# Batched 90-degree rotation on one core: one 8 KB-row slab at each end of the order instead of two at the start, and stores that are not held back

## The chip, the cores and the metric

The kernel runs on one core of a Trainium2 chip. The metric is the time of one execution on the device, in microseconds (us). The kernel before takes 122.95 us, the median of three runs (122.94 to 122.95).

## The reference

The input is a batch of 32 x 3 images of 256 x 256 float32 values, 25.17 MB. Every image is turned by 90 degrees clockwise:

```python
def reference(x):
    return np.rot90(x, k=-1, axes=(-2, -1)).astype(np.float32)
```

Nothing is calculated. Each value is read from HBM (the chip's main memory) once and written back once, elsewhere: 50.33 MB in all.

## The kernel before

All images together are 24,576 rows of 256 values (1 KB each). The kernel cuts them into twelve **slabs** of 2,048 rows, 2 MB each, which is 16 KB on each of the 128 partitions of SBUF (the on-chip memory). All twelve slabs have a place of their own in SBUF, so that no buffer is used twice. The slabs form five **groups** of `sizes = (2, 2, 2, 4, 2)` slabs, in the tiles `groups[0]` to `groups[4]`.

**Loads.** SP, an engine that here only issues transfers, issues every load and every store, in the order of the program, into a single queue. Group 0 is loaded in a form of its own (lines 52 to 56): its two slabs lie as rows of 8 KB on each partition. The second slab comes first, as two transfers of 1 MB (line 55), then the first slab as one transfer of 2 MB (line 56). Groups 1 to 4 are loaded by lines 57 to 66 with rows of 16 KB (32 KB in group 3), one transfer of 2 MB per slab. The last of them is cut into two of 1 MB: line 63, whose instruction is kept in the variable `mark`, and line 64. That makes 14 loads.

**Turning.** VectorE (DVE in the profile) turns the data with its transpose instruction, 24 times 128 partitions x 2,048 values. `turn_slab` (lines 68 to 72) handles the two slabs of group 0 with two transposes each. The slab that comes first is turned into the two halves of `spare`, which lie in PSUM (a small second memory of the core); the other one is turned into the place that the first has left (lines 75 and 76). ScalarE (ACT) then copies `spare` into the place that the second slab has left (line 78). `turn_group` (lines 80 to 98) turns a group of slabs in place: a quarter of the data is transposed into a side buffer, `extra` or `spare` (line 88), the other three quarters inside the group's own tile (line 93), and ACT copies the side buffer back (line 98).

**Stores.** Each group leaves in two transfers, one with the even partitions and one with the odd ones (lines 104 to 113): 2 MB each, 4 MB each in group 3. That makes 10 stores. The first store has an extra dependency on `mark` (lines 107 to 109): SP waits in front of it until the load of line 63 has landed.

All instructions of SP run in order: what stands behind a waiting instruction waits too. The framework gives the transfers eight completion counters (semaphores) in turn, and each transfer waits until the one eight places ahead of it, which used the same counter, has landed.

Of the kernel before, what the change touches and what calls it, by code (L numbers as in the profile page):

```python
# [1 line left out]

# [4 lines left out]


@with_exitstack  # L10
def kernel(
    ctx: ExitStack,
    tc: tile.TileContext,
    x: bass.AP,
    out: bass.AP,
):

    nc = tc.nc
    fp32 = mybir.dt.float32

    B, C, H, W = x.shape
    P = nc.NUM_PARTITIONS
    R = 16  # L30
    E = R * W
    hw = R // 2
    low, high = slice(0, hw), slice(hw, R)

    rows_in = x.rearrange("b c h w -> (b c h) w")
    rows_out = out.rearrange("b c h w -> (b c h) w")

    sizes = (2, 2, 2, 4, 2)
    first = [sum(sizes[:n]) for n in range(len(sizes))]
    groups = [  # L40
        ctx.enter_context(tc.tile_pool(name=f"group{n}", bufs=1)).tile([P, s, E], fp32, name=f"u{n}")
        for n, s in enumerate(sizes)
    ]
    psum = ctx.enter_context(tc.tile_pool(name="psum", bufs=1, space=bass.MemoryType.PSUM))
    spare = [psum.tile([P, E // 2], fp32, name=f"spare{h}") for h in range(2)]
    extra = ctx.enter_context(tc.tile_pool(name="extra", bufs=1)).tile([P, E // 2], fp32, name="extra")

    def rows_of(rows, n):
        return rows[first[n] * P * R : (first[n] + sizes[n]) * P * R]


    ld = rows_of(rows_in, 0).rearrange("(s i p r) w -> s i p (r w)", s=2, i=2, p=P)
    home = [groups[0][:, s].rearrange("p (i f) -> p i f", i=2) for s in range(2)]
    for i in range(2):
        nc.sync.dma_start(out=home[0][:, i], in_=ld[1, i])  # L55
    nc.sync.dma_start(out=home[1], in_=ld[0].transpose([1, 0, 2]))
    for n in range(1, len(sizes)):
        I = sizes[n]
        ld = rows_of(rows_in, n).rearrange("(a i m r) w -> i m a (r w)", a=2, i=I, m=P // I)
        to = groups[n].rearrange("p s f -> p (s f)").rearrange("p (a f) -> p a f", a=2)  # L60
        for i in range(I):
            if (n, i) == (len(sizes) - 1, I - 1):
                mark = nc.sync.dma_start(out=to[i::I, 0], in_=ld[i][:, 0])
                nc.sync.dma_start(out=to[i::I, 1], in_=ld[i][:, 1])
            else:
                nc.sync.dma_start(out=to[i::I], in_=ld[i])

    def turn_slab(src, dsts):
        s = src.rearrange("p (i r g c) -> p c r g i", i=2, r=R // 2, c=R)
        for h, d in enumerate(dsts):  # L70
            d = d.rearrange("p (c k r) -> p c r k", c=hw, r=R // 2)[:, :, ::-1, ::-1]
            nc.vector.transpose(out=d, in_=s[:, h * hw : (h + 1) * hw])  # L72

    u = groups[0]
    turn_slab(u[:, 0], spare)
    turn_slab(u[:, 1], [u[:, 0, : E // 2], u[:, 0, E // 2 :]])
    for h in range(2):
        nc.scalar.copy(out=u[:, 1, h * E // 2 : (h + 1) * E // 2], in_=spare[h])  # L78

    def turn_group(n, held):  # L80
        I = sizes[n]
        T = I // 2
        K = W // (R * T)
        u = groups[n].rearrange("p s f -> p (s f)")
        src = u.rearrange("p (a t r g c) -> p t c r g a", a=2, t=T, r=R, c=R)
        dst = u.rearrange("p (i c k t r) -> p t c r k i", i=I, c=R, k=K, t=T)[:, ::-1, :, ::-1, ::-1, :]
        for t in range(T):
            nc.vector.transpose(  # L88
                out=held[t].rearrange("p (i c k r) -> p c r k i", i=I, c=hw, k=K)[:, :, ::-1, ::-1, :],
                in_=src[:, t, low, low])  # L90
        for c, r in ((low, high), (high, high), (high, low)):
            for t in range(T):
                nc.vector.transpose(out=dst[:, t, c, r], in_=src[:, t, c, r])  # L93
        back = u.rearrange("p (i c k t r) -> p t i c k r", i=I, c=R, k=K, t=T)[:, ::-1]
        for t in range(T):
            kept = held[t].rearrange("p (i c k r) -> p i c k r", i=I, c=hw, k=K)
            for i in range(I):
                nc.scalar.copy(out=back[:, t, i, low, :, high], in_=kept[:, i])  # L98

    for n, held in enumerate(([extra], [spare[1]], spare, [extra]), 1):  # L100
        turn_group(n, held)


    st = rows_of(rows_out, 0).rearrange("(s i m r) w -> i m s (r w)", s=2, i=2, m=P // 2)
    for a in range(2):
        put = nc.sync.dma_start(out=st[a], in_=groups[0][a::2])
        if a == 0:
            tc.add_manual_dep(put.ins, mark.ins.name, mybir.DependencyInfo(
                mybir.DependencyClass.Sync, mybir.DependencyReason.SCHED_ONLY), reason="stores after loads")
    for n in range(1, len(sizes)):  # L110
        st = rows_of(rows_out, n).rearrange("(a i m r) w -> a m i (r w)", a=2, i=sizes[n], m=P // 2)
        for a in range(2):
            nc.sync.dma_start(out=st[a], in_=groups[n][a::2])


# [1 line left out]
_INS = ['x']  # L117
_OUTS = [((32, 3, 256, 256), 'float32')]


# [23 lines left out]
```

## Time and profile before

| what | value |
|---|---|
| median of the runs shown | 122.95 us (122.94 to 122.95) |
| the profiled execution's own time | 122.88 us |
| its span, first to last instruction | 121.1 us |
| VectorE busy | 87.4 us in 24 instructions |
| ScalarE busy | 14.9 us in 17 instructions |
| moved by the 16 DMA engines | 50.33 MB, 416 GB/s over the span |
| line 72, transposes into `spare` | 2, mean 3,586 ns |
| line 72, transposes into the group's tile | 2, mean 3,988 ns |
| line 78, copies by ScalarE from `spare` | 2, mean 1,870 ns |
| line 98, copies by ScalarE from a side buffer | 14, mean 605 to 1,043 ns by shape |

The profile page names an engine, a line, an operation and its tiles in each row, then how many there were and how long they took. The span is cut into 40 slices of 3 us, with a digit for each engine's busy share in tenths and the GB/s that the DMA engines moved. Other views of the same trace give the instructions in order of time, the waits by engine, and busy times in chosen stretches; "share" of the DMA there is the mean over the 16 DMA engines. "SPq" is the sequencer of SP, where the transfers are issued: an issue takes half a microsecond or so, and the transfer lands much later.

### The profile page before, as it was taken

Reading aid. Unit: us, or ns where it says so; the run is one execution under the profiler, and the core shown is the slowest. Engines: PE = TensorE matmul, PEld = TensorE weight load, DVE = VectorE, ACT = ScalarE, POOL = GpSimd, SP = SyncE. Lnnn points to the kernel's source line nnn. Section 1 sums busy time; section 2 is a strip of 40 time slices with the busy share of each in tenths; the row PEclk is TensorE's granted clock in tenths of the full one; section 3 lists DMA queues with packets and bytes.
Section 4 is the critical chain, followed back from the end, with each engine's and each line's share of the span. In section 5 each row is a group of like instructions: output and inputs, shape, how many; then the busy total and the mean of one; then the engine's idle time right before and its main releaser. Section 6 shows DMA issues by size and latency. Waiting matters only on the chain.

```text
span 121.1 us, 131 instructions
## 1 busy us (share of the span) xinstructions
DVE 87.4 (72%) x24; ACT 14.9 (12%) x17; POOL 0.2 (0%) x4
## 2 busy tenths in 40 slices
DVE  0039999999999999999999999999999600000000
ACT  0000400380005100060000000318000330000000
POOL 0000000000000000000000000000000000000000
DMA  2999999999989898999999999999999999999994
GB/s 89 428 428 422 452 433 433 433 433 433 520 346 520 346 520 346 428 422 411 433 433 428 433 433 428 417 417 433 428 433 433 433 433 433 433 433 433 433 422 184
DMA packets 3456, 50.33 MB, mean 416 GB/s; under 512 B 384, under 2 KB 384, under 8 KB 384
## 3 DMA queue, kind: packets, MB, share of 16 engines
q1 hardware_dynamic: 3456, 50.33, 97.6%
HBM read 25.17 MB, written 25.17 MB: 416 GB/s over the span
## 4 chain that ended last, share of the span: by engine, by line
DVE 66%; issue 6%; DMA 6%; ACT 1%; ACTq 1%; SPq 0%; DVEq 0%
DVE u L93 39%; DVE spare L88 9%; DVE extra L88 6%; DVE u L72 6%; DVE spare L72 6%; DMA u<-in_x_dram 6%; ACT u L98 1%; ACTq L139 1%; SPq L55 0%; DVEq L88 0%; DVEq L72 0%
## 5 line engine op out<-in xcount | busy, mean ns | idle before, releaser
L93 DVE STREAM_TRANSPOSE u<-u 128x2048 f32<-128x2048 f32 x15 | 54.4, 3649 | 0.4
L72 DVE STREAM_TRANSPOSE spare<-u 128x2048 f32<-128x2048 f32 x2 | 7.1, 3586 | 8.1 <-DMA u<-in_x_dram 8.1
L98 ACT COPY u<-spare 128x512 f32<-128x512 f32 (+1 forms) x10 | 6.0, 687 | 38.5 <-DVE u L93 38.5
L88 DVE STREAM_TRANSPOSE spare<-u 128x2048 f32<-128x2048 f32 x3 | 10.7, 3588 | 0.0
L72 DVE STREAM_TRANSPOSE u<-u 128x2048 f32<-128x2048 f32 x2 | 7.8, 3988 | 0.0
L88 DVE STREAM_TRANSPOSE extra<-u 128x2048 f32<-128x2048 f32 x2 | 7.8, 3896 | 0.0
L98 ACT COPY u<-extra 128x1024 f32<-128x1024 f32 x4 | 4.0, 1043 | 22.8 <-DVE u L93 22.8
L78 ACT COPY u<-spare 128x2048 f32<-128x2048 f32 x2 | 3.6, 1870 | 8.7 <-DVE u L72 8.7
L78 ACT ACT_TABLE_LOAD x1 | 1.3, 1283 | 13.0 <-DMA u<-in_x_dram 13.0
L128 POOL MEMSET const-uint8-127<- 128x1 uint8 x1 | 0.1, 103 | 0.0
L128 POOL MEMSET const-bfloat16-1.0<- 128x1 bf16 x1 | 0.1, 102 | 0.0
L128 POOL MEMSET const-float32-0.0<- 128x1 f32 x1 | 0.1, 99 | 0.2 <-issue 0.2
L128 POOL MEMSET const-float32-1.0<- 128x1 f32 x1 | 0.1, 99 | 0.0
## 6 DMA issues: line engine op xcount, KB each, us to landing
u<-in_x_dram SPq DMA_DIRECT2D x10, 2048.0 KB, 30.4
out_dram<-u SPq DMA_DIRECT2D x8, 2048.0 KB, 18.2
out_dram<-u SPq DMA_DIRECT2D x2, 4096.0 KB, 21.1
u<-in_x_dram SPq DMA_DIRECT2D x4, 1024.0 KB, 20.5
```

The costliest lines, as they stand in the source:

```text
L72: nc.vector.transpose(out=d, in_=s[:, h * hw : (h + 1) * hw])
L78: nc.scalar.copy(out=u[:, 1, h * E // 2 : (h + 1) * E // 2], in_=spare[h])
L88: nc.vector.transpose(out=held[t].rearrange("p (i c k r) -> p c r k i", i=I, c=hw, k=K)[:, :, ::-1, ::-1, :], in_=src[:, t, low, low])
L93: nc.vector.transpose(out=dst[:, t, c, r], in_=src[:, t, c, r])
L98: nc.scalar.copy(out=back[:, t, i, low, :, high], in_=kept[:, i])
L128: nc = _bacc.Bacc("TRN2", target_bir_lowering=False, num_devices=1)
L139: with _tile.TileContext(nc) as tc:
```

## The change

The twelve slabs are grouped as `(1, 2, 2, 4, 2, 1)`. The first and the last group hold one slab each in the form with 8 KB rows; the first is loaded as two transfers of 1 MB and the last as one of 2 MB. Both are turned into the two halves of `spare`, and ScalarE copies them back into their own place, where before only one of two slabs went that way. The last load of 16 KB rows is no longer cut in two. The dependency of the first store on `mark` is gone. The two single slabs are stored as two transfers of 1 MB each.

```diff
-    sizes = (2, 2, 2, 4, 2)
+    sizes = (1, 2, 2, 4, 2, 1)
...
+    for n, I in enumerate(sizes):
+        u = groups[n].rearrange("p s f -> p (s f)")
+        if I == 1:
+            ld = rows_of(rows_in, n).rearrange("(i p r) w -> i p (r w)", i=2, p=P)
+            to = u.rearrange("p (i f) -> p i f", i=2)
+            if n:
+                nc.sync.dma_start(out=to, in_=ld.transpose([1, 0, 2]))
+            else:
+                for i in range(2):
+                    nc.sync.dma_start(out=to[:, i], in_=ld[i])
+            continue
+        ld = rows_of(rows_in, n).rearrange("(a i m r) w -> i m a (r w)", a=2, i=I, m=P // I)
+        to = u.rearrange("p (a f) -> p a f", a=2)
+        for i in range(I):
+            nc.sync.dma_start(out=to[i::I], in_=ld[i])
-    ld = rows_of(rows_in, 0).rearrange("(s i p r) w -> s i p (r w)", s=2, i=2, p=P)
-    home = [groups[0][:, s].rearrange("p (i f) -> p i f", i=2) for s in range(2)]
-    for i in range(2):
-        nc.sync.dma_start(out=home[0][:, i], in_=ld[1, i])
-    nc.sync.dma_start(out=home[1], in_=ld[0].transpose([1, 0, 2]))
...
-            if (n, i) == (len(sizes) - 1, I - 1):
-                mark = nc.sync.dma_start(out=to[i::I, 0], in_=ld[i][:, 0])
-                nc.sync.dma_start(out=to[i::I, 1], in_=ld[i][:, 1])
...
+    def turn_slab(n):
+        u = groups[n][:, 0]
+        s = u.rearrange("p (i r g c) -> p c r g i", i=2, r=R // 2, c=R)
+        for h in range(2):
+            d = spare[h].rearrange("p (c k r) -> p c r k", c=hw, r=R // 2)[:, :, ::-1, ::-1]
             nc.vector.transpose(out=d, in_=s[:, h * hw : (h + 1) * hw])
-    u = groups[0]
-    turn_slab(u[:, 0], spare)
-    turn_slab(u[:, 1], [u[:, 0, : E // 2], u[:, 0, E // 2 :]])
-    for h in range(2):
-        nc.scalar.copy(out=u[:, 1, h * E // 2 : (h + 1) * E // 2], in_=spare[h])
+        for h in range(2):
+            nc.scalar.copy(out=u[:, h * E // 2 : (h + 1) * E // 2], in_=spare[h])
...
+    turn_slab(0)
     for n, held in enumerate(([extra], [spare[1]], spare, [extra]), 1):
         turn_group(n, held)
+    turn_slab(len(sizes) - 1)
...
-    for a in range(2):
-        put = nc.sync.dma_start(out=st[a], in_=groups[0][a::2])
-        if a == 0:
-            tc.add_manual_dep(put.ins, mark.ins.name, mybir.DependencyInfo(
-                mybir.DependencyClass.Sync, mybir.DependencyReason.SCHED_ONLY), reason="stores after loads")
+            st = rows_of(rows_out, n).rearrange("(a m r) w -> a m (r w)", a=2, m=P // 2)
+            for a in range(2):
+                nc.sync.dma_start(out=st[a], in_=groups[n][a::2, 0])
+            continue
```

More of the change, by code (lines that the diff above doesn't have):

```diff
@@ L49, in rows_of @@
         return rows[first[n] * P * R : (first[n] + sizes[n]) * P * R]
-    ld = rows_of(rows_in, 0).rearrange("(s i p r) w -> s i p (r w)", s=2, i=2, p=P)
-    home = [groups[0][:, s].rearrange("p (i f) -> p i f", i=2) for s in range(2)]
-    for i in range(2):
-        nc.sync.dma_start(out=home[0][:, i], in_=ld[1, i])
-    nc.sync.dma_start(out=home[1], in_=ld[0].transpose([1, 0, 2]))
-    for n in range(1, len(sizes)):
-        I = sizes[n]
+    for n, I in enumerate(sizes):
[9 more added lines that the diff above has]
+            continue
@@ L59 @@
         ld = rows_of(rows_in, n).rearrange("(a i m r) w -> i m a (r w)", a=2, i=I, m=P // I)
-        to = groups[n].rearrange("p s f -> p (s f)").rearrange("p (a f) -> p a f", a=2)
+        to = u.rearrange("p (a f) -> p a f", a=2)
         for i in range(I):
-            if (n, i) == (len(sizes) - 1, I - 1):
[L63 to L71, printed above, removed]
-            nc.vector.transpose(out=d, in_=s[:, h * hw : (h + 1) * hw])
-    u = groups[0]
-    turn_slab(u[:, 0], spare)
-    turn_slab(u[:, 1], [u[:, 0, : E // 2], u[:, 0, E // 2 :]])
-    for h in range(2):
-        nc.scalar.copy(out=u[:, 1, h * E // 2 : (h + 1) * E // 2], in_=spare[h])
+            nc.sync.dma_start(out=to[i::I], in_=ld[i])
@@ L98, in turn_group @@
                 nc.scalar.copy(out=back[:, t, i, low, :, high], in_=kept[:, i])
+    turn_slab(0)
     for n, held in enumerate(([extra], [spare[1]], spare, [extra]), 1):
         turn_group(n, held)
-    st = rows_of(rows_out, 0).rearrange("(s i m r) w -> i m s (r w)", s=2, i=2, m=P // 2)
-    for a in range(2):
-        put = nc.sync.dma_start(out=st[a], in_=groups[0][a::2])
-        if a == 0:
-            tc.add_manual_dep(put.ins, mark.ins.name, mybir.DependencyInfo(
-                mybir.DependencyClass.Sync, mybir.DependencyReason.SCHED_ONLY), reason="stores after loads")
-    for n in range(1, len(sizes)):
-        st = rows_of(rows_out, n).rearrange("(a i m r) w -> a m i (r w)", a=2, i=sizes[n], m=P // 2)
+    turn_slab(len(sizes) - 1)
+    for n, I in enumerate(sizes):
+        if I == 1:
+            st = rows_of(rows_out, n).rearrange("(a m r) w -> a m (r w)", a=2, m=P // 2)
+            for a in range(2):
+                nc.sync.dma_start(out=st[a], in_=groups[n][a::2, 0])
+            continue
+        st = rows_of(rows_out, n).rearrange("(a i m r) w -> a m i (r w)", a=2, i=I, m=P // 2)
         for a in range(2):
```

## The prediction

> **What bounds the kernel now.** I read the page first: busy rows, the DMA row, the queue and the chain.
>
> ```profile
> DVE 87.4 (72%) x24; ACT 14.9 (12%) x17; POOL 0.2 (0%) x4
> ...
> DMA  2999999999989898999999999999999999999994
> ...
> q1 hardware_dynamic: 3456, 50.33, 97.6%
> ...
> DVE 66%; issue 6%; DMA 6%; ACT 1%; ACTq 1%; SPq 0%; DVEq 0%
> ```
>
> The chain names VectorE, but its shares add up to 80%: it ends with the issue of the last stores, and the last fifth of the span, in which their data still moves, isn't in it. The DMA row and the queue's 97.6% name the real bound. The stretches (DVE, ACT, POOL busy, clock, DMA share, GB/s) show where the missing 2.4% lies:
>
> ```profile
> 59.00:63.00 4.00, 3.97 (x3) 0.00 (x0) 0.00 (x0) 1.00 1.01 430
> 63.00:97.00 34.00, 32.71 (x9) 5.19 (x10) 0.00 (x0) 1.00 1.00 427
> 97.00:118.00 21.00, 0.00 (x0) 0.91 (x1) 0.00 (x0) 1.00 1.02 432
> ```
>
> Further stretches of this view have a DMA share of 0.13 up to 1.9 us and of 0.00 from 120.0 us on. Between the two the engines never pause, not even at 59 to 63, where loads give way to held stores. Next, SP's waits and the issues in time:
>
> ```profile
> SPq L106 <- DMA u<-in_x_dram: 31.2, 1, 31.2
> ```
> ```profile
> 12.95 0.60 SPq L66 DMA_DIRECT2D u<-in_x_dram  x1
> ...
> 17.84 0.61 SPq L66 DMA_DIRECT2D u<-in_x_dram  x1
> ...
> 22.75 0.51 SPq L63 DMA_DIRECT2D u<-in_x_dram  x1
> 27.64 0.49 SPq L64 DMA_DIRECT2D u<-in_x_dram  x1
> ...
> 59.43 1.37 SPq L106 DMA_DIRECT2D out_dram<-u  x2
> ```
>
> Each of these four loads waits for the landing eight places ahead of it, so the issues are a clock of landings: 4.89 us per 2 MB of 16 KB rows (17.84 to 22.75 to 27.64), and 4.97 for the 8 KB slab (first slab landed 7.98, second 12.95). Line 63 lands 36.5 us after its issue (59.25), line 64 34.1 us after (61.74): 2.49 us for 1 MB. The last store lands 21.7 us after its issue at 98.6: 120.3. From 7.98 to 120.3 move 23 slabs' worth, 112.3 / 23 = 4.88 each. The time is the queue's bytes; all else only has to keep ahead of it.
>
> How far ahead it is, from VectorE's and ScalarE's instructions in time:
>
> ```profile
> 22.84 3.91 DVE L88 STREAM_TRANSPOSE extra<-u 128x2048 f32<-128x2048 f32 x1
> ...
> 81.04 3.88 DVE L88 STREAM_TRANSPOSE extra<-u 128x2048 f32<-128x2048 f32 x1
> ```
> ```profile
> 81.19 3.03 ACT L98 COPY u<-spare 128x512 f32<-128x512 f32 x6 [2.69 <-DVE u L93]
> 95.92 1.99 ACT L98 COPY u<-extra 128x1024 f32<-128x1024 f32 x2 [11.70 <-DVE u L93]
> ```
>
> Group 3, the large one, is ready at 84.2. The queue runs dry without it after all loads and six 2 MB stores: 61.74 + 6 x 4.88 = 91.0. Cover 6.8 us; for group 4 (ready 97.9, needed at 110.6) 12.7 us.
>
> **The change, part by part.**
>
> *Loads.* Thirteen instead of fourteen: two of 1 MB, ten of 2 MB with long rows, one 8 KB slab. The bytes per row form are the same (two slabs of 8 KB, six of 16 KB, four of 32 KB); the 4.97 us slab moves from second place to last. Only the cut of the last 16 KB load goes. A cut costs 2.49 - 4.89 / 2 = 0.045 us; the pair at the start (0.73 + 4.8 = 5.5 and 7.98, so 2.4 to 2.5 us each, against 4.97) says between -0.03 and nothing. I take 0.045, nearest in row length and partitions (64): -0.045. Loads end at 61.7, as before.
>
> *Stores.* Twelve instead of ten: group 0's two of 2 MB become four of 1 MB, +2 x 0.045 = +0.09. No store of 1 MB is in the trace; the bounds are the same -0.03 and +0.045 each. Net of both lines +0.045, between -0.1 and +0.1.
>
> The Trainium skill speaks against this: "SBUF — State Buffer", section "The DMA setup-cost knee", has every transfer pay about 2 us whatever its size, and asks for the largest transfers on 128 partitions. By it one transfer more is an estimated +2.0 us, about 125. The trace has 2.49 us for a whole 1 MB transfer on 64 partitions, so behind a full queue the fixed part isn't paid in time.
>
> *The hold.* Its 31.2 us of waiting vanish from SP. They cost nothing now, as the loads already queued kept the engines full (share 1.01 at 59 to 63, 430 GB/s against 431 in the stretch of loads from 8 to 59: at most 1/431 of 4 us, 0.01 us). Without it the first store waits only for its data (about 19) and its counter, eight places back (the sixth load, 27.6); the second 32.5, group 1's 37.4 and 42.2, group 2's 49.1 and 52, group 3's 79.3, group 4's 93, the last 101.7. The last load is issued at 22.75, when the fifth has landed, so no load stands behind a waiting store on SP, and in the queue the stores stand behind all loads. Price: nothing, as long as the queue serves in order.
>
> *VectorE.* First slab at 8.06, two transposes, done 15.1. Group 1's second load is now the fourth and lands at 17.75 instead of 22.75; VectorE idles 2.7 us and starts at 17.85, 5.0 earlier than the 22.84 above. Then the old spacings (group 1 14.8 us, group 2 14.5, group 3 28.9, group 4 14.9): group 2 done at 47.1, group 3 at 76.1 with copies to 79.3, group 4 at 90.9 with copies to 93.0. The last slab: 7.1 us to 98.0, and its two copies (3.7 us, both behind both transposes, whose source they overwrite) to 101.7. Busy time falls by 7.8 - 7.1 = 0.7 us, ScalarE's grows by 3.7; both off the path. Group 3's last load lands at 47.1, just when VectorE wants it: a delay there comes off the cover first.
>
> *Cover after.* Without group 3 the queue holds the loads and five 2 MB of stores: dry at 61.7 + 5 x 4.88 = 86.1, against 79.3: 6.8 us. Group 4: 105.6 against 93.0. Last slab: 115.4 against 101.7, 13.7 us. If group 3's cover went, each us of delay would cost one.
>
> *Sum.* Profiled execution 122.88 = 1.8 outside the span + 121.1. Plus 0.045: 122.93. The median shown is 0.07 above this execution: **123.0 us**.
>
> **Rivals.**
>
> *Stores get between loads (slower).* Either the queue serves stores beside queued loads, or the build puts some ahead of them. From 27.6 on, up to one 2 MB store then enters per landed load: ahead of group 3's last load come group 0's stores (4.9) and group 1's (9.8), so it lands 14.6 later and group 3 is ready at 93.9. The queue has nothing but group 3 left at 86.1, and stands still for 7.8 us: **130.8**. It decides once that load is more than 6.8 us late. For it: the trace never shows stores queued behind several loads, and the program has no dependency left that keeps them apart. Against: the two stores issued at 59.43 stood behind line 64's load, which landed in its own 2.49 us, and up to eight queued loads landed one after another at 4.9 us.
>
> *Mixed traffic runs slower (slower).* Stores stand in the queue from 27.6 to 61.7 beside loads. If that stretch ran at 427 GB/s, the lowest above, instead of 431: 34.1 x 4 / 431 = 0.32 us more, **123.3**. For it: no row has reads and writes queued together for more than a few us. Against: both directions queued together at 59 to 63 ran at 430.
>
> *The early queue helps (faster).* If the stores' stretch of 34 us at 427 reached 432, the best of the store stretches (97 to 118): 0.4 us, **122.6**. Against: the engines have no pause there, and a longer queue gives a busy engine nothing.
>
> **How the numbers follow.** A difference within 0.2% (0.25 us) I call no change. My forecast, 123.0: 0.68. Stores between loads, or another lost cover: 0.11. Slower mixed traffic: 0.15. Faster: 0.06. So faster 0.06, same 0.68, slower 0.26. The forecast's own range is 122.85 to 123.15 (the bounds of -0.1 and +0.1). For 8 in 10 the range reaches down to 122.8 and up past the mixed-traffic case to 123.5; 130.8 stays outside.
>
> **What would show it.** Right: one load landing per 4.9 us until 61.7; SP's 31.2 us wait gone and first store issued near 27.6, yet landing near 64; group 3's stores issued near 79; VectorE idle 2.7 us before group 1 and done near 98; queue share still 97 to 98%. Wrong: a load of group 3 landing after 54, a slice of the DMA row under 9 near 86, or a landing step in the mixed stretch above 4.95 us. The forecast falls if any pause opens in the queue.

## The result, and the profile after

The changed kernel takes 123.61 us, the median of six runs (123.34 to 123.81), beside 122.94 us for the kernel before, measured with it. The ratio is 1.0053, with a 95% interval of 1.0038 to 1.0067: slower by about half a percent. The profiled execution took 123.81 us, the longest of the six, with a span of 122.0 us, 0.9 us more than the span before.

The page of the changed kernel, the lines that answer to those of before:

```profile
DVE 86.7 (71%) x24; ACT 18.6 (15%) x19; POOL 0.2 (0%) x4
...
DMA  3999999999999999999999999999999999999993
GB/s 118 416 454 430 430 430 430 430 473 430 430 430 430 430 430 392 424 430 408 344 397 435 430 430 435 435 430 435 430 430 435 430 430 430 430 430 440 435 430 140
...
q1 hardware_dynamic: 3472, 50.33, 97.4%
...
DMA 38%; DVE 33%; issue 6%; DVEq 3%; ACT 2%; ACTq 1%; SPq 0%
```

The DMA row shows nines in all slices but the first and the last: by busy time nothing is wrong. The row below it has the loss. Around the 20th slice (58 to 61 us) the engines are as busy as ever and move 344 GB/s. The chain now names the DMA with 38%, but that is group 3's last load on its way: it lands at 47.1, just when VectorE wants it, so the chain follows it back through the queue. It again ends with the last issue, and it doesn't show where the time went.

The stretches of the changed kernel (length, DVE, ACT, POOL busy, clock, DMA share, GB/s):

```profile
8.00:57.00 49.00, 45.86 (x13) 7.55 (x6) 0.00 (x0) 1.00 1.00 429
57.00:62.70 5.70, 5.67 (x3) 0.00 (x0) 0.00 (x0) 1.00 1.02 359
62.70:119.50 56.80, 35.17 (x10) 9.73 (x12) 0.00 (x0) 1.00 1.01 432
```

The same stretches of the kernel before:

```profile
8.00:57.00 49.00, 48.69 (x14) 8.84 (x7) 0.00 (x0) 1.00 1.01 433
57.00:62.70 5.70, 5.67 (x2) 0.00 (x0) 0.00 (x0) 1.00 0.97 414
62.70:119.50 56.80, 33.01 (x10) 6.10 (x10) 0.00 (x0) 1.00 1.01 429
```

The loss lies in the middle stretch, the **handover**, where the loads end and the stores begin: (414 - 359) x 5.7 / 430 = 0.73 us of transfer. (The 429 beside 433 in the first stretch is no loss of the loads: by the completion times in the two traces, the ten loads of 2 MB after the first slab took 48.79 us here and 48.86 before.) The DMA share at the handover is 1.02, and that is the trap: packets that take longer count as busy for longer. A packet is one piece of a transfer that one engine moves. From 59.5 to 61.5 us single 8 KB packets in the trace took up to 0.75 us instead of 0.31 (one took 0.97).

SP's waits for loads at the stores (lines 105 and 109 of the changed kernel), its issues in time, and the landing of the last load (line 56):

```profile
SPq L109 <- DMA u<-in_x_dram: 10.6, 3, 4.3
...
SPq L105 <- DMA u<-in_x_dram: 8.7, 2, 4.5
```
```profile
22.79 0.40 SPq L56 DMA_DIRECT2D u<-in_x_dram  x1
27.75 5.30 SPq L105 DMA_DIRECT2D out_dram<-u  x2
```
```profile
DMA to landing us min/median/max: 40.0/40.0/40.0
```

The wait of 31.2 us is gone; what is left of SP's waits for loads at the stores are at most 4.5 us each, for a counter. The first two stores are issued at 27.75 and some 5 us later, where before SP waited until 59.43. The last load lands at 22.79 + 40.0 = 62.8. From the completion times in the trace, the load ahead of it landed at 56.89, so this one took 5.93 us; the same form took 4.97 us near the start of the kernel before. All other loads of 2 MB still land 4.85 to 4.90 us apart.

VectorE's instructions in time:

```profile
17.98 3.92 DVE L83 STREAM_TRANSPOSE extra<-u 128x2048 f32<-128x2048 f32 x1 [2.71 <-DMA u<-in_x_dram]
...
94.34 3.63 DVE L71 STREAM_TRANSPOSE spare<-u 128x2048 f32<-128x2048 f32 x1
```

It idles 2.71 us before group 1 and is done at 97.97. The last stores are issued at 101.7, far ahead of the queue.

### The profile page after: what moved, and what is told of

Same layout as the page of the kernel before. It is cut to its first block, busy times and chain, and to the rows that moved or that the text cites. A ratio compares the mean times of both kernels' runs of the same rounds, so it can differ in the third digit from the quotient of the medians.

```text
span 122.0 us, 134 instructions
## 1 busy us (share of the span) xinstructions
DVE 86.7 (71%) x24; ACT 18.6 (15%) x19; POOL 0.2 (0%) x4
## 4 chain that ended last, share of the span: by engine, by line
DMA 38%; DVE 33%; issue 6%; DVEq 3%; ACT 2%; ACTq 1%; SPq 0%
DMA u<-in_x_dram 38%; DVE u L88 18%; DVE spare L71 6%; DVE spare L83 6%; DVE extra L83 3%; DVEq L135 3%; ACT u L73 2%; ACTq L135 1%; SPq L59 0%; DVEq L83 0%
## 5 line engine op out<-in xcount | busy, mean ns | idle before, releaser
L88 DVE STREAM_TRANSPOSE u<-u 128x2048 f32<-128x2048 f32 x15 | 54.6, 3664 | 0.4
L71 DVE STREAM_TRANSPOSE spare<-u 128x2048 f32<-128x2048 f32 x4 | 14.3, 3593 | 8.2 <-DMA u<-in_x_dram 8.2
L83 DVE STREAM_TRANSPOSE spare<-u 128x2048 f32<-128x2048 f32 x3 | 10.6, 3578 | 0.0
L73 ACT COPY u<-spare 128x2048 f32<-128x2048 f32 x4 | 7.3, 1870 | 9.9 <-DVE spare L71 9.9
```

Of the source, the lines that this page charges most:

```text
L73: nc.scalar.copy(out=u[:, h * E // 2 : (h + 1) * E // 2], in_=spare[h])
L83: nc.vector.transpose(out=held[t].rearrange("p (i c k r) -> p c r k i", i=I, c=hw, k=K)[:, :, ::-1, ::-1, :], in_=src[:, t, low, low])
```

## The experiments

Three theories were open. S: stores that stand in the queue behind the loads slow the end of the loads. R: the 8 KB slab is slow as the last load by itself. C: it takes both. Times are medians, ratios are to the kernel before, run beside each kernel, which took 123.00 or 123.01 us. Landings, distances between them and packet times come from the completion times and packets in one profiled execution of each run. That execution isn't always a typical one: it was the longest of its run in the changed kernel and in runs 1, 2 and 5, and the shortest in runs 4, 8 and 11.

**1. A hold on the last load (`e1_hold_last`).**

```diff
-                nc.sync.dma_start(out=to, in_=ld.transpose([1, 0, 2]))
+                mark = nc.sync.dma_start(out=to, in_=ld.transpose([1, 0, 2]))
...
+                if n == 0 and a == 0:
+                    tc.add_manual_dep(put.ins, mark.ins.name, ...)
```

> The changed kernel with a hold put back: its first store waits until the whole last load (the 8 KB slab) has landed, so no store is queued while it moves. In the changed kernel this load landed 5.93 us after the one before it, against 4.97 for the same form in the kernel before. Theory S (stores queued behind the loads slow the last load): it lands 4.9 to 5.0 us after the one before; the gain of 0.96 us is given back by a pause of 1.5 to 2.5 us before the first store, so 124.0 to 125.5 us in all. Theory R (8 KB rows, or this slab's place in memory, are slow in this position by themselves): it still lands 5.9 us after, and the pause comes on top, 125 to 126. Theory C (only both together are slow): as S.

Measured: 123.78 us (123.11 to 124.20, 9 runs), ratio 1.0051 (1.0034 to 1.0068); the last load took 5.71 us. The time is below what any of the three theories expected. The slow load looks like theory R, but the profile shows that it need not be:

```profile
27.69 35.39 SPq L105 DMA_DIRECT2D out_dram<-u  x2
```

Two issues, of which one at 27.69: the framework put the pair's second store, which has no dependency, ahead of the held one. So one store of 1 MB stood behind the loads after all. The run says that one is enough for the loss; it doesn't separate the theories. Run 7 holds every store.

**2. The kernel before without its hold (`e2_before_nohold`).**

```diff
-        if a == 0:
-            tc.add_manual_dep(put.ins, mark.ins.name, mybir.DependencyInfo(
-                mybir.DependencyClass.Sync, mybir.DependencyReason.SCHED_ONLY), reason="stores after loads")
```

> The kernel before without the dependency of its first store on line 63; all else as it was, so the loads end with 16 KB rows while stores are queued behind them. Theory S: the last load of 1 MB lands 3.0 to 3.5 us after the one before it instead of 2.45, and the time is 123.4 to 124. Theory R: no change, 122.9 to 123.0. Theory C: no change.

Measured: 123.30 us (123.16 to 123.54, 9 runs), ratio 1.0023 (1.0014 to 1.0032). The last load of 1 MB, in 16 KB rows, landed 3.18 us after the one before it instead of 2.45. The stretch around it, in this run, in the kernel before and in the changed kernel:

```profile
59.50:61.50 2.00, 2.00 (x1) 0.00 (x0) 0.00 (x0) 1.00 0.97 262
```
```profile
59.50:61.50 2.00, 2.00 (x1) 0.00 (x0) 0.00 (x0) 1.00 0.93 393
```
```profile
59.50:61.50 2.00, 2.00 (x1) 0.00 (x0) 0.00 (x0) 1.00 1.07 266
```

The same dip as in the changed kernel, at 0.97 of busy time, with nothing changed but the hold. Theory S holds for the load; R and C, which expected no change, fall as the whole cause. The median lies 0.1 us under the range of S: it rose by 0.3 us, while the profiled execution, with 123.54 us the longest of the nine, lost 0.73 us at the handover.

**3. The last slab in 16 KB rows (`e3_last_16k`).**

```diff
-                nc.sync.dma_start(out=to, in_=ld.transpose([1, 0, 2]))
+                ld = rows_of(rows_in, n).rearrange("(p r) w -> p (r w)", p=P)
+                nc.sync.dma_start(out=u, in_=ld)
```

> The changed kernel with the last slab loaded as 16 KB rows, each partition from one place, in the same single transfer of 2 MB; nothing is held. The values of this slab lie in other places of the tile, so the last slab of the output is not the turned image; all transfers, transposes and copies are as many and as large as before. Theory S: the last load still lands 5.9 us after the one before, 123.6 us. Theory R and theory C: 4.9 us, and 122.6 to 122.9 us.

Measured: 123.32 us (123.23 to 123.73, 11 runs), ratio 1.0030 (1.0021 to 1.0040); the last load took 5.47 us instead of 4.89. The loss is there without 8 KB rows. It was smaller than theory S expected (5.9 us, 123.6) and than in the changed kernel (0.58 us against 0.96), which raised the question of runs 9 and 10.

**4. The cut and the hold put back (`e4_split_hold`).**

```diff
-                nc.sync.dma_start(out=to, in_=ld.transpose([1, 0, 2]))
+                mark = nc.sync.dma_start(out=to[:, 0], in_=ld[0])
+                nc.sync.dma_start(out=to[:, 1], in_=ld[1])
```

with the first store held on `mark`, as before.

> The changed kernel with the kernel before's way to hand over: the last slab is loaded as two transfers of 1 MB, and the first store waits until the first of the two has landed. Theory S: the stores reach the queue only when the first half has landed, so the first half lands after 2.45 us and the second loses at most a part, 122.7 to 123.2 us in all. Theory R: both halves together take 5.9 us, 123.6 us. Theory C: as S.

Measured: 122.97 us (122.79 to 123.15, 11 runs), ratio 0.9996 (0.9988 to 1.0005). Both halves land after 2.48 us. The stores are issued here:

```profile
59.23 1.19 SPq L106 DMA_DIRECT2D out_dram<-u  x2
```

With the hold the whole loss is gone, though slabs, turns and the number of stores are those of the change.

**5. A hold released 2 MB ahead (`e5_hold_2mb`).** All stores wait for the load ahead of the last.

```diff
-            nc.sync.dma_start(out=to[i::I], in_=ld[i])
+            mark = nc.sync.dma_start(out=to[i::I], in_=ld[i])
...
+    def held(put):
+        tc.add_manual_dep(put.ins, mark.ins.name, ...)
```

> The changed kernel with every store held until group 4's last load has landed, the load ahead of the last: stores reach the queue 4 to 5 us before the loads end. In the run with one 1 MB store queued the last load landed 5.71 us after the one before it; with stores queued 2.4 us ahead (split load) nothing was lost. Theory L (a store in the queue while more than some 2.3 us of loads are still to come costs 0.6 to 1.0 us at the handover, whatever else is queued): last load 5.6 to 5.9 us after the one before, 123.4 to 123.8 us. Rival D (the loss comes from a deep queue of stores built up over 30 us): 4.9 to 5.0 us, 122.9 to 123.1.

Measured: 123.28 us (123.08 to 123.50, 7 runs), ratio 1.0023 (1.0011 to 1.0035); the last load took 5.47 us.

```profile
57.12 1.19 SPq L109 DMA_DIRECT2D out_dram<-u  x2
```

Stores issued from 57.1 on are already too early; a queue of stores 30 us deep isn't needed. Rival D falls. Theory L had the direction and too high a price: 5.6 to 5.9 us and 123.4 to 123.8.

**6. Three handovers (`e6_three_turns`).** Dependencies that only order the issues give: nine loads, two stores, two loads, two stores, two loads, the rest.

```diff
+    order = [(stores, 0, 0), (stores, 0, 1), (loads, 3, 3), (loads, 4, 0),
+             (stores, 1, 0), (stores, 1, 1), (loads, 4, 1), (loads, 5, 0), (stores, 2, 0), (stores, 2, 1)]
+    for (x, n, a), (y, m, b) in zip(order, order[1:]):
+        tc.add_manual_dep(y[m, b].ins, x[n, a].ins.name, ...)
```

> The changed kernel with another order on the queue, nothing held: after nine loads come the first slab's two stores, then two loads, group 1's two stores, the last two loads, and the other stores. Loads give way to stores three times instead of once, and stores to loads twice. Bytes and transfers are the same, VectorE's cover falls to 1 to 2 us but holds. Theory L: each of the three handovers costs 0.6 to 1.0 us, so 1.2 to 2.0 us more than the changed kernel, 124.8 to 125.6, and more if stores giving way to loads cost too; the load ahead of each turn lands 0.6 to 1.0 us late. Rival E (only the end of all loads is slow, where the queue holds no further load): no more than 0.2 us over the changed kernel, 123.4 to 123.8. Both assume that the queue serves in order: if stores overtook loads, the landings would not follow the issues.

Measured: 124.50 us (124.31 to 124.71, 4 runs), ratio 1.0126 (1.0110 to 1.0142), 0.9 us over the changed kernel. The load ahead of the first handover landed 1.00 us late (5.86 for 4.86), ahead of the second 0.53 us (5.42 for 4.89), ahead of the third not at all (4.93 for an 8 KB slab). So the loss isn't tied to the last load, and rival E falls; but theory L, which wanted it at each of the three, is right for two, and the time lies 0.3 us below its range. Loads that follow stores lost nothing: the last store ahead of the first turn back landed 0.36 us late, the load behind it 0.33 us early. Landings followed the issues throughout, so nothing overtook.

**7. Everything held until the last load has landed (`e7_hold_all_last`).** As run 1, with the hold on every store.

> The changed kernel with every store held until the whole last load has landed (in the earlier run of this kind one store of 1 MB slipped past the hold, issued at 27.7). Theory L and rivals D and E: the last load lands 4.9 to 5.0 us after the one before, and the first store lands 1.5 to 2.5 us later than 2.45 us after it, a pause without any transfer: 124.3 to 125.3 us. If the 8 KB rows are slow in this place by themselves, the last load still takes 5.5 us or more.

Measured: 125.26 us (125.16 to 125.31, 4 runs), ratio 1.0184 (1.0170 to 1.0198). The stretches:

```profile
57.00:59.50 2.50, 2.50 (x2) 0.00 (x0) 0.00 (x0) 1.00 1.01 423
59.50:61.50 2.00, 2.00 (x1) 0.00 (x0) 0.00 (x0) 1.00 0.77 320
61.50:63.50 2.00, 1.97 (x2) 0.00 (x0) 0.00 (x0) 1.00 0.31 131
63.50:65.50 2.00, 2.00 (x2) 0.00 (x0) 0.00 (x0) 1.00 0.94 393
```

Here the share falls with the GB/s, to 0.31: this is a true pause, the picture that I had looked for in the wrong case. The 8 KB slab as the last load took 4.95 us, so it isn't slow in that place by itself (theory R, a second time). The first store landed 4.26 us later instead of 2.45, a pause of 1.8 us. The pause isn't all of it: the next four stores, of 2 MB, land 4.91 to 4.94 us apart, where the changed kernel's stores of 2 MB land 4.84 to 4.88 apart, and from the last load's landing on this run needs 2.2 us more than the kernel before.

**8. A hold released 0.5 MB ahead (`e8_hold_half_mb`).** The second half of the last slab is cut again, by even and odd partitions, and all stores wait for the even part.

```diff
+                nc.sync.dma_start(out=to[:, 0], in_=ld[0])
+                mark = nc.sync.dma_start(out=to[0::2, 1], in_=ld[1][0::2])
+                nc.sync.dma_start(out=to[1::2, 1], in_=ld[1][1::2])
```

> The changed kernel with the last slab loaded in three transfers (1 MB, then 0.5 MB of the even and 0.5 MB of the odd partitions) and every store held until the first 0.5 MB has landed, so stores are issued 1.2 us before the loads end. Theory L: no slow load packets; the first store's issue of some 0.6 us and its way to the engines take longer than what is left, a pause of 0 to 1 us: 122.9 to 123.9 us, not better than with 1 MB of lead (122.97).

Measured: 124.05 us (123.97 to 124.08, 4 runs), ratio 1.0086 (1.0072 to 1.0100). No slow load packets; the first store landed 3.08 us after the last load, a pause of 0.6 us. The estimate for the pause held, but the time lies 0.15 us above its upper end: as in run 7 the stores of 2 MB behind the pause land further apart (4.90 to 4.93 us for the first four), which the estimate left out and which stays unexplained.

**9 and 10. The row form, side by side (`e9_after_again`, `e10_last_16k_again`).** The changed kernel and run 3, both unchanged.

> The changed kernel as it is, a second time, beside the next run. The handover with everything queued early cost 0.96 us where the last load has 8 KB rows (123.61 us) and 0.57 us where the same bytes come as 16 KB rows (123.32 us), in different sessions. Theory A (8 KB rows make the handover dearer): again 123.5 to 123.7 us, 0.2 us or more above the next run. Rival V (the loss varies from one execution to the next, and the row form has no part in it): within 0.1 us of the next run.

> The changed kernel with the last slab loaded as 16 KB rows, again (that slab's values lie in other places, so its part of the output is not the turned image; the transfers are the same in number and bytes). Theory A: 123.2 to 123.4 us, 0.2 us or more below the run before this. Rival V: within 0.1 us of it.

Measured: 123.48 us (123.43 to 123.86, 5 runs), ratio 1.0044 (1.0030 to 1.0057) with 8 KB rows, and 123.61 us (123.45 to 123.66, 5 runs), ratio 1.0047 (1.0033 to 1.0061) with 16 KB rows. The last loads took 5.66 and 5.69 us. The difference between the changed kernel and run 3 did not come again: the row form has no part in it that these runs can tell. Run 3 and run 10 are the same kernel and differ by 0.29 us. The distance of the medians here (0.13 us) is a little more than rival V allowed, in the other direction from theory A.

**11. The cut without the hold (`e11_split_nohold`).** Run 4 without its dependency: the last slab comes in two loads of 1 MB, and nothing is held.

> The changed kernel with the last slab loaded as two transfers of 1 MB, nothing held: the run that came out at 122.97 us, but without its hold. If the hold is what keeps the handover free, and not the cut: the second half lands 3.0 to 3.5 us after the first instead of 2.48, and 123.3 to 123.7 us in all. If the cut does it: 2.4 to 2.5 us and 122.9 to 123.1.

Measured: 123.62 us (123.60 to 123.82, 5 runs), ratio 1.0054 (1.0041 to 1.0066); the second half landed after 3.23 us. The first two stores, and the stretch of the dip:

```profile
32.49 5.31 SPq L106 DMA_DIRECT2D out_dram<-u  x2
```
```profile
59.50:61.50 2.00, 2.00 (x1) 0.00 (x0) 0.00 (x0) 1.00 1.11 348
```

It is the hold, not the cut: run 4 differs by the dependency alone and takes 122.97.

**12. A hold released 1.5 MB ahead (`e12_hold_1_5_mb`).** The first half of the last slab is cut by even and odd partitions, and all stores wait for the even part.

```diff
+                mark = nc.sync.dma_start(out=to[0::2, 0], in_=ld[0][0::2])
+                nc.sync.dma_start(out=to[1::2, 0], in_=ld[0][1::2])
+                nc.sync.dma_start(out=to[:, 1], in_=ld[1])
```

> The changed kernel with the last slab loaded in three transfers (0.5, 0.5 and 1 MB) and every store held until the first has landed, 3.7 us before the loads end. Holds released 1.2, 2.4 and 4.9 us ahead gave 124.05, 122.97 and 123.28 us, and slow load packets began some 2 to 2.5 us before the loads' end. Theory L: stores are in the queue some 2.5 to 3 us ahead, so a part of the loss shows: 123.0 to 123.3. If any store issued more than a little early cost the whole 0.5 to 1 us: 123.3 to 123.6.

Measured: 122.91 us (122.80 to 123.07, 11 runs), ratio 0.9990 (0.9981 to 0.9999), just below the kernel before, and the lowest of all. No slow packet is left:

```profile
58.15 1.16 SPq L111 DMA_DIRECT2D out_dram<-u  x2
```
```profile
59.50:61.50 2.00, 2.00 (x1) 0.00 (x0) 0.00 (x0) 1.00 1.10 459
```

The expectation of a partial loss was wrong: a first store issued 3.6 us ahead of the loads' end costs nothing, one issued 5.4 us ahead (run 5) delays the last load by 0.5 us. The two runs also differ in how the last slab is cut (three loads here, one in run 5), and no run tells this apart from the lead. The runs with one handover in one table, ordered by how long before the last load's landing the first store was issued (landings from the trace's completion times; "late" is the last load against the same form undisturbed, for the 8 KB slab the 4.95 us of run 7, for 2 MB in 16 KB rows 4.89; "cut" means that the last 2 MB came as two loads of 1 MB):

```
kernel              first store ahead   last load late   pause after   median
changed, e9         35 us               0.98, 0.71       -             123.61, 123.48
e1 (one store)      35                  0.76             -             123.78
e3, e10 (16 KB)     35                  0.58, 0.80       -             123.32, 123.61
e11, e2 (cut)       30                  0.75, 0.73       -             123.62, 123.30
e5                   5.4                0.52             -             123.28
e12                  3.6                0                -             122.91
e4, before           2.4, 2.3           0                -             122.97, 123.0
e8                   1.2                0                0.6           124.05
e7                  -0.1                0                1.8           125.26
```

## Why the prediction was wrong, point by point

The forecast was 123.0 us within 122.8 to 123.5, and no change with 0.68; measured were 123.61 and slower.

- **The hold: this step failed.** I wrote that the 31.2 us of waiting "cost nothing now" and that without them the price is "nothing, as long as the queue serves in order". The queue did serve in order, in every run, and the price was 0.7 to 1.0 us at the handover in the profiles of the changed kernel, and 0.5 to 0.7 us in its medians. The working looked only at what the wait costs SP (0.01 us) and not at what it keeps away. Pairs that differ by the dependency alone settle it: the kernel before against run 2, and run 4 against run 11. That the hold is the cause is shown; what happens inside the engines while loads and stores change over isn't.
- **Evidence that I read too far.** Line 64's load landed in what I read as its own 2.49 us (2.45 by the completion times) with two stores issued at 59.43 behind it, and I took that as proof that queued stores don't disturb loads. The table says that the lead was short enough (2.3 us). The row did not reach the case at hand, where the lead is 35 us. The DMA share of 1.01, with which I argued that the engines were kept full, can't show such a loss either.
- **The rivals.** Stores between loads (130.8) did not come: loads landed every 4.85 to 4.90 us until 56.9. Slower mixed traffic had the right sign and, with 123.3, about the right size by luck, but the wrong place: I spread 0.32 us over the 34 us in which both kinds are queued, while the stretch from 8 to 57 shows no slower load, and all is lost in the last 2 to 2.5 us of the loads. My upper end of 123.5 rested on its price of 0.32 us, less than half of what the handover lost.
- **The moved 8 KB slab, priced at nothing: right.** As last load it took 4.95 us when nothing stood behind it (run 7), and 8 KB and 16 KB rows lose alike (runs 9 and 10).
- **Cuts and small stores, +0.045 us net: too dear, if anything.** The 0.045 came from two times to landing that the view rounds to 0.1 us; by the completion times the two halves took 4.92 us together, beside 4.85 to 4.92 for uncut loads of 16 KB rows, so the cut cost nothing that can be seen. The 1 MB stores landed 2.41 to 2.45 us apart, half of a 2 MB store's 4.84 to 4.88. The 2.0 us estimated from the skill's "SBUF — State Buffer", section "The DMA setup-cost knee", did not show in a full queue.
- **VectorE, ScalarE and the covers: right.** Idle before group 1 2.7 us (measured 2.71), done at 98.0 (97.97), last copies to 101.7 (101.6), busy time 0.7 us less on VectorE and 3.7 us more on ScalarE (3.6). The framework moved one of the last slab's transposes ahead of group 4's last one, which I had not foreseen. Group 4's first store was issued at 96.5 instead of 93 for it; the queue came to it at 106.6, so this cost nothing.
- **The sum, from the completion times of the two profiled executions.** Start 0.13 us later, loads after the first slab +0.95 us, stores -0.20 us (58.34 against 58.54 for the twelve slabs): +0.88, and the span grew by 0.9. The loss at the handover is nearly the whole of the loads' term. The other two terms I had at zero. The start, whose loads are the same in all runs, differs between them by some 0.4 us (second load landed at 7.88 to 8.26), so it isn't put down to the change; the slightly faster stores remain unexplained.
- **What would show it.** I had named "a landing step in the mixed stretch above 4.95 us" as a sign of error, and it came, at 5.93. "If any pause opens in the queue" never came: the loss had the form of slow packets, which a share of busy time can't show.

The Trainium skill, "DMA: Bandwidth & Descriptors", section "Rules for kernel authors", advises, for overlapping a transfer with compute, to issue it early and to wait for it late. For stores behind loads in a full queue, earliest was not best here: with the first store issued about 30 us or more ahead of the loads' end the kernels took 123.3 to 123.8 us, with 2.3 to 3.6 us 122.9 to 123.0. No run here issues the loads later.

## What to carry to other kernels

Where one queue of transfers is the bound, look at GB/s beside the busy share, stretch by stretch: in this kernel a handover from loads to stores lost 0.5 to 1 us at full "busy". Where loads all come first, try a hold of the stores on a load that ends 1 to 1.5 MB before the last (here 2.3 to 3.6 us ahead). In these runs less opened a pause (0.6 us with 0.5 MB, 1.8 us with none), and 2 MB or no hold brought the slow packets back. Check in the trace that no store slips past the hold, as in run 1. All of this is one kernel on one core; where the limits lie in another has to be measured there. Before a wait is priced at nothing, ask what it keeps out of the queue, and look for a row in which that stands there for as long as it will.

## What the runs showed of the hardware

- Loads slow down before the first store's packets show. In the changed kernel the slow packets begin at 59.5 us and the first 16 KB store packet starts at 61.4; one queued store of 1 MB, with all others kept behind the held one, is enough (run 1, 0.76 us).
- The loss isn't won back: behind each slow end the next transfers land at their usual distance (2.45 us for the 1 MB stores of the changed kernel).
- The engines mostly fall apart at a lossy handover: the time between the first and the last of the 16 engines' completions of one transfer grew from 0.65 to 1.0 us in the changed kernel, and stayed there to the end; in run 12 it went from 0.46 to 0.52. But in run 2, with 0.73 us lost, it grew only from 0.60 to 0.72.
- The size of the loss varies (0.5 to 1.0 us in the profiled executions, 0.3 to 0.7 in the medians of the kernels without any hold), and the third handover of run 6, at which that spread was already 1.1 us, lost nothing, though its first store had been issued 28.7 us ahead. Whether the spread is the reason wasn't tried, and neither was where between 3.6 and 5.4 us of lead the loss sets in.
